# Two-layer diffusion backbone: context row gathers held beside the first layer's pair selection and table, and 72 in place of 56 u chunks ahead of the dense stage

## The chip, the cores and the metric

The kernel runs on one core of one Trainium2 chip. Its engines are TensorE (PE), VectorE (DVE), ScalarE (ACT) and GpSimd (POOL); SyncE (SP) issues most transfers. The metric is device time in microseconds for one execution of the whole program.

## The reference, cut to what matters

512 latent tokens and 256 context tokens of width 1024 go through two layers. Each layer is a mixer (attention, a gating MLP, Fourier mixing, gates), then an expert retrieval. The second layer's attention reads keys and values of the context too, so it needs what the context's retrieval in the first layer gives.

```python
q = rms_unit((t @ w_q).reshape(T, 8, 2, 128))
s = einsum('thpc,hpkc->thpk', q, sub_keys)
s1, i1 = top_k(s[:, :, 0], 16); s2, i2 = top_k(s[:, :, 1], 16)
# 256 pairs of each head -> the best 16 pairs: idx = i1 * 128 + i2, g = softmax(scores)
act = gelu(einsum('td,thkd->thk', t, u_tab[idx]))
out = einsum('thk,thkd->td', g * act, v_tab[idx])     # 16384 rows of 1024 in each table
```

## The kernel before

**Two ways to do the retrieval.** For the first layer's 512 latent tokens the kernel does it densely: all 128 chunks of 128 table rows are multiplied with the tokens (`dense_u`, then gelu), the result is multiplied with a table of pair weights that `gtable` writes to DRAM, and the product goes through the 128 chunks of v (`dense_v`). For the 256 context tokens it gathers rows instead: two blocks of 128 tokens with 128 pairs each, first all rows of u, then all rows of v. These are four jobs (block 0 u, block 0 v, block 1 u, block 1 v) of 128 steps.

**How gathers are paced.** `step()` (L836) issues one indirect transfer of 128 rows (512 KB) on POOL's queue into one of four row buffers and, three steps later (LAG), uses a row on DVE: a product summed into a column of dots for u (L867), a multiply-add into acc for v (L876). Each use is tied behind the DVE instruction that was the latest when it was traced. `pace(cols)` (L827) is called behind every group of three matmuls and adds cols / 2.4 ns to `owed`; each 1700 ns of it is one step. `spend()` (L833) takes 1800 ns away for each 512 KB tile loaded (0.4 of that for a spilled chunk read back), down to -7200. `finish()` (L881) issues all steps that are left at once.

**Order of the first layer's expert part.** `interleave` (L145) advances generators in rounds. Here they are: the second layer's conditioning columns (`ada`, 24 loads, 0.4 a round), the rest of the context's routing (`cr`), `routing()` (1 a round: 8 rounds of norm, 8 of `route1`, one for each head, and 32 of `route2`, 8 for each of four blocks), `table()` (1 a round; block b starts when `route2` has done it, so its 32 rounds begin in the last round of the first block and end 7 rounds after `route2`), and `fill()` (FILL[0] a round, once the norm is done). `fill()` makes u chunks ahead of the dense stage: SPILL[0][0] + NGS - LEAD of them, 40 + 16 - 2 = 54; two more follow before the dense loop, 56 in all. Forty of the 56 are spilled: written to DRAM (`gsd`) and read back in `dense_v`. SPILL[0] = (40, 3) spills every third chunk. What `fill()` has not made when the rounds end, it makes alone. The dense loop then makes 128 v chunks and the other 72 u chunks, one behind each v chunk that is not a spilled one.

**The second layer.** Its mix (Fourier, then the gating MLP: 36 rounds) is interleaved with `context()` (L1085), with the gates of two branches (16 weight tiles, 0.6 a round) and with 16 conditioning loads (1.2 a round). `context()` waits until the last context row is used or mix has ended; then it calls `finish()`, adds the rows' sum to the context, norms it and writes ctx.H and ctx.L. Behind the interleave comes `qkv` (L503), with K first: `projN` (L350) loads four weight tiles and multiplies each with the four latent blocks, whose accumulators fill all four ps banks, and with the two context blocks (px banks). The split weight tiles have three buffers.

Of the kernel before, what the change touches and what calls it, by code (L numbers as in the profile page):

```python
# [47 lines left out]
STEPS = ((1700, 1700, 1700), (1700, 1700, 1700))  # L48
LAG = 3
NGSS = (16, 30)  # L50
SPILL = ((40, 3), (40, 3))
FILL = (1.0, 1.3)
LEAD = 2
ADA = 6
WBUFS = ((3, 2), (3, 4))
# [22 lines left out]
class Ker:  # L78
    def __init__(self, tc, a, es):
        self.tc, self.nc, self.a, self.es = tc, tc.nc, a, es  # L80
        self.uid, self.turn, self.banks = 0, False, PBANKS
        self.wp = self.wb = self.wr = None
        self.jobs, self.flight, self.owed, self.every = [], [], 0, STEPS[0][0]


    def pool(self, es, name, bufs=1, space=None, side=None):
# [738 lines left out]
        self.jobs.append({"l": l, "r": r, "tab": tab, "next": 0})  # L825

    def pace(self, cols):  # L827
        self.owed += cols / 2.4
        while self.owed >= self.every:
            self.owed -= self.every  # L830
            self.step()
# [103 lines left out]
    @staticmethod  # L935
    def spilled(l, c):
        n, m = SPILL[l]
        return c % m == m - 1 and c // m < n

    def dense_u(self, l, c, sp, up, hH, hL, tag, bufs):  # L940
# [9 lines left out]
        if spill:  # L950
            nc.sync.dma_start(self.gsd[c // SPILL[l][1]], gS)
        return gS

    def dense_v(self, l, c, vp, sp, gS, gd, accs, acc7, between):
# [12 lines left out]
        if self.spilled(l, c):  # L967
            gS = vp.tile([P, TD], F32, tag="gSr", name=self.nm("gSr"), bufs=2)
            nc.sync.dma_start(gS, self.gsd[c // SPILL[l][1]])
            self.spend(0.4)  # L970
# [28 lines left out]
    def layer(self, l, xin, cin, xfin, rin):  # L999
        nc, a, tc, two = self.nc, self.a, self.tc, self.two  # L1000
        last = l == DEPTH - 1
# [5 lines left out]
        gd = dt("gd", [TD // GT, P, NK * GT])  # L1007
        self.gsd = dt("gsd", [SPILL[l][0], P, TD])
        cm = cfin = None
# [173 lines left out]
        def ahead(n):  # L1183
            while len(gSs) < n:
                c = order[len(gSs)]
                gSs[c] = self.dense_u(l, c, self.pp, up, dH, dL, "ps", self.banks["ps"])
                yield
        with ExitStack() as e:
            rp = self.pool(e, f"rp{l}")
            for b in range(4):  # L1190
                for n in ("i1", "i2", "g"):
                    if n not in rx[b]:
                        rx[b][n] = rp.tile([P, P], F32, name=f"{n}x{l}_{b}")
            gt, normed = [], []

            def routing():
                with ExitStack() as e2:
                    tmp = self.pool(e2, f"rn{l}")
                    yield from self.norm(tmp, l, xm, SEQ, 1, 0, lambda k: (dH[:, k, :], dL[:, k, :]), r1)
                    normed.append(True)  # L1200
                with ExitStack() as e2:
                    tmp = self.pool(e2, f"rt{l}")
                    yield from self.route1(l, tmp, rp, SimpleNamespace(H=dH, L=dL, T=SEQ), (tmp, *PQB))
                with ExitStack() as e2:
                    tmp = self.pool(e2, f"nat{l}")
                    for b in range(NDB, 4):
                        self.natural(tmp, rx[b]["hnd"], dH, dL, b)
                gt.append(self.pool(e, f"gt{l}"))
                yield from self.route2(gt[0], list(range(NDB, 4)) + list(range(NDB)), rx, l)

            def table():
                for b in range(NDB):
                    while "done" not in rx[b]:
                        yield
                    yield from self.gtable(gt[0], b, rx[b], gd)

            def fill():
                while not normed:
                    yield
                yield from ahead(SPILL[l][0] + NGS - LEAD)  # L1220
            self.interleave((self.ada(*((l, range(10, 12)) if last else (l + 1, range(ADA))), None, "fl"), 4 * AN[l]),
                            (None if last else cr, CR2), (routing(), 1), (table(), 1), (fill(), FILL[l]))
        epp.close()

        self.every = STEPS[l][2]
        with ExitStack() as e:
            vp = self.pool(e, f"dv{l}")
            acc7 = vp.tile([P, TD], F32, name=f"da{l}_7")
            with ExitStack() as e2:
# [3 lines left out]
                self.added = {}  # L1233
                room = [SPILL[l][0] + NGS]

# [170 lines left out]
```

## Time and profile before

| | us |
|---|---|
| median of three runs | 4993.69 |
| lowest run | 4987.19 |
| the profiled execution | 4982.3 |
| its span, from first to last instruction | 4980.5 |

Shares of the span: PE 91%, DVE 68%, POOL 41%, ACT 38%. The chain that ended last is PE for 57%, DVE 15%, DMA 8%. The first layer's expert part runs from about 1100 to 2895 us, and the second layer's mix from 2947 to 3148. Matmul ends are modelled and successive matmuls overlap, so the spacing of matmuls says more than their mean length. In the rows, du and d, da are the matmuls of the u and v chunks, px of the table (and the context's accumulators in the second layer), idxc the indices of the context's rows.

### The profile page before, as it was taken

What the parts mean: (1) busy time and instruction counts of PE and PEld (TensorE: products, weight loads), DVE (VectorE), ACT (ScalarE), POOL (GpSimd) and SP (SyncE); (2) the same over time, 40 slices, a digit from 0 to 9 for tenths busy, and PEclk for the clock granted to TensorE, in tenths of its full rate; (3) what the DMA queues carried; (4) which work ended last, traced back from release to release, by engine and by line L of the source; (5) the groups of instructions that cost most, each with busy time, mean ns of one, the idle gap of its engine ahead of it and who ended that gap; (6) DMA issues with size and microseconds to landing.
All of it is one profiled execution on the core that took longest, in us unless ns stands there. A gap on an engine that the chain in (4) does not pass through costs nothing.

```text
span 4980.5 us, 65298 instructions
## 1 busy us (share of the span) xinstructions
PE 4521.8 (91%) x23501; PEld 3851.7 (77%) x23501; DVE 3366.8 (68%) x6818; ACT 1910.4 (38%) x3201; POOL 2029.4 (41%) x1246
## 2 busy tenths in 40 slices
PE   7899988789789899999899989989897899999998
PEld 4787777667667788877778767767787788999998
DVE  3115485868888667766777874457459976777787
ACT  2222444322578522222222233334334783333332
POOL 1011012335655565655556420111225665555531
PEclk9999999989999999999999999999999899999999
DMA  4442245556567889988889886333536668888986
GB/s 167 144 135 68 92 134 167 170 174 217 200 223 247 297 285 318 318 290 273 272 294 303 306 267 204 101 96 110 170 92 192 214 241 297 293 289 301 302 287 228
DMA packets 447508, 1092.84 MB, mean 219 GB/s; under 512 B 37200, under 2 KB 193744, under 8 KB 440016
## 3 DMA queue, kind: packets, MB, share of 16 engines
q1 hardware_dynamic: 336592, 685.97, 42.2%
q0 software_dynamic: 110592, 402.70, 23.6%
q8 instruction: 185, 3.03, 0.2%
q14 instruction: 139, 1.14, 0.1%
HBM read 970.04 MB, written 118.49 MB: 219 GB/s over the span
## 4 chain that ended last, share of the span: by engine, by line
PE 57%; DVE 15%; issue 8%; DMA 8%; POOL 5%; ACT 4%; SPq 0%; POOLq 0%; DVEq 0%; ACTq 0%
PE du L113 6%; PE du L115 5%; PE du L114 5%; PE da L114 5%; PE da L113 5%; PE da L115 5%; PE ps L113 3%; PE ps L114 3%; PE ps L115 3%; DMA row<-in_u_dram,idxc 2%; POOL row L848 2%; PE px L929 2%; DVE row L867 2%; PE px L113 2%; PE px L115 2%
## 5 line engine op out<-in xcount | busy, mean ns | idle before, releaser
L109 POOL TENSOR_TENSOR wL<-wraw,wH 128x1024 fp32r<-128x1024 f32 x291 | 714.9, 2458 | 1138.9 <-ACT wH L102 1053.4
L102 ACT ACTIVATE wH<-wraw 128x1024 fp32r<-128x1024 f32 x460 | 486.7, 1059 | 1155.2 <-PE du L114 319.5
L113 PE MATMUL du<-dH,wH 128*128 128x512 f32 (+1 forms) x2048 | 781.5, 382 | 64.5 <-DVE da L990 45.5
L115 PE MATMUL du<-dH,wL 128*128 128x512 f32 (+1 forms) x2048 | 774.1, 378 | 43.8 <-DVE wL L109 22.6
L114 PE MATMUL du<-dL,wH 128*128 128x512 f32 (+1 forms) x2048 | 769.5, 376 | 6.5 <-DVE dL L335 6.5
L113 PE MATMUL da<-AH,vH 128*128 128x512 f32 (+1 forms) x1792 | 647.3, 363 | 7.8 <-ACT AH L102 7.8
L114 PE MATMUL da<-AL,vH 128*128 128x512 f32 (+1 forms) x1792 | 651.1, 363 | 0.7 <-DVE AL L109 0.6
L115 PE MATMUL da<-AH,vL 128*128 128x512 f32 (+1 forms) x1792 | 650.5, 363 | 0.0
L867 DVE SCALAR_TENSOR_TENSOR row<-row,hn 128x1024 f32<-128x1024 f32 x384 | 508.6, 1345 | 103.6 <-DMA row<-in_u_dram,idxc 89.8
L102 ACT ACTIVATE vH<-vr 128x1024 fp32r<-128x1024 f32 x256 | 271.7, 1062 | 779.6 <-PE da L114 550.1
L876 DVE SCALAR_TENSOR_TENSOR acc<-row,dots,acc 128x1024 f32<-128x1024 f32 x381 | 501.2, 1315 | 7.6 <-DMA row<-in_v_dram,idxc 3.7
L113 PEld LDWEIGHTS du<-dH,wH 128*128 128x128 f32 x2048 | 399.9, 195 | 123.1 <-DVE da L990 56.2
L848 POOL DMA_INDIRECT row<-in_v_dram,idxc x256 | 327.8, 1280 | 406.1 <-DVE acc L876 354.7
L115 PEld LDWEIGHTS du<-dH,wL 128*128 128x128 f32 x2048 | 400.2, 195 | 94.2 <-DVE wL L109 27.1
L848 POOL DMA_INDIRECT row<-in_u_dram,idxc x256 | 334.2, 1305 | 324.1 <-DVE row L867 228.4
L114 PEld LDWEIGHTS du<-dL,wH 128*128 128x128 f32 x2048 | 400.0, 195 | 47.5 <-DVE dL L335 9.0
L109 DVE TENSOR_TENSOR wL<-wraw,wH 128x1024 fp32r<-128x1024 f32 x169 | 220.8, 1307 | 269.0 <-ACT wH L102 256.4
L990 DVE TENSOR_TENSOR da<-d,da 128x512 f32<-128x512 f32 (+1 forms) x254 | 158.1, 622 | 333.3 <-PE d L115 332.8
L113 PEld LDWEIGHTS da<-AH,vH 128*128 128x128 f32 x1792 | 337.8, 189 | 43.9 <-ACT AH L102 8.5
L114 PEld LDWEIGHTS da<-AL,vH 128*128 128x128 f32 x1792 | 338.0, 189 | 37.7 <-DVE AL L109 2.4
L115 PEld LDWEIGHTS da<-AH,vL 128*128 128x128 f32 x1792 | 338.0, 189 | 35.3
L109 DVE TENSOR_TENSOR vL<-vr,vH 128x1024 fp32r<-128x1024 f32 x256 | 326.2, 1274 | 50.9 <-ACT vH L102 49.2
(385 smaller groups left out, 9441.9 us busy)
## 6 DMA issues: line engine op xcount, KB each, us to landing
wraw<-in_uT_dram SPq DMA_DIRECT2D x256, 512.0 KB, 4.6
vr<-in_v_dram SPq DMA_DIRECT2D x256, 512.0 KB, 6.1
wraw<-in_wt_dram SPq DMA_DIRECT2D x204, 512.0 KB, 3.7
gd<-stg SPq DMA_DIRECT2D x56, 1024.0 KB, 5.4
araw<-in_wada_dram SPq DMA_DIRECT2D x96, 512.0 KB, 4.4
gt<-gd SPq DMA_DIRECT2D x16, 2048.0 KB, 18.0
gt<-gd SPq DMA_DIRECT2D x16, 1536.0 KB, 12.4
gatex<-g SPq DMA_DIRECT2D x48, 256.0 KB, 2.1
```

What stands on the lines that cost most here:

```text
L102: nc.scalar.activation(H, src, AF.Copy)
L109: e.tensor_tensor(L, src, H.bitcast(F32), op=ALU.subtract)
L113: nc.tensor.matmul(out, aH, bH, start=start, stop=False)
L114: nc.tensor.matmul(out, aH, bL, start=False, stop=False)
L115: nc.tensor.matmul(out, aL, bH, start=False, stop=stop)
L848: nc.gpsimd.indirect_dma_start(out=row, out_offset=None, in_=self.a[f"{job['tab']}{job['l']}"], in_offset=bass.IndirectOffsetOnAxis(ap=r[" ...
L867: nc.vector.scalar_tensor_tensor(row, row, 1.0, job["hn"], op0=ALU.mult, op1=ALU.mult, accum_out=dots[:, j:j + 1])
L876: nc.vector.scalar_tensor_tensor(job["acc"], row, dots[:, j:j + 1], job["acc"], op0=ALU.mult, op1=ALU.add)
L929: nc.tensor.matmul(gp[:, j * P:(j + 1) * P], ob[:, j, :], oa[:, j, :], start=True, stop=True)
L990: add = nc.vector.tensor_tensor(acc7, s[:, :TD], acc7, op=ALU.add)
```

## The change

- While `held` is set, `pace` returns at once: nothing is added to `owed` and no step is issued; `spend` still takes away. It is set in the first layer when `route1` is done, and cleared when the last table block is traced. The second layer doesn't hold.
- SPILL[0] goes from (40, 3) to (56, 2): every second chunk is spilled, 56 in all, so `fill()` makes 56 + 16 - 2 = 70 chunks, with two more before the loop; 56 u chunks are left for the loop.
- FILL[0] goes from 1.0 to 1.3 chunks a round.

```diff
--- before.py
+++ after.py
@@ -48,8 +48,8 @@
 STEPS = ((1700, 1700, 1700), (1700, 1700, 1700))
 LAG = 3
 NGSS = (16, 30)
-SPILL = ((40, 3), (40, 3))
-FILL = (1.0, 1.3)
+SPILL = ((56, 2), (40, 3))
+FILL = (1.3, 1.3)
 LEAD = 2
 ADA = 6
 WBUFS = ((3, 2), (3, 4))
@@ -81,6 +81,7 @@
         self.uid, self.turn, self.banks = 0, False, PBANKS
         self.wp = self.wb = self.wr = None
         self.jobs, self.flight, self.owed, self.every = [], [], 0, STEPS[0][0]
+        self.held = False
 
 
     def pool(self, es, name, bufs=1, space=None, side=None):
@@ -825,6 +826,8 @@
         self.jobs.append({"l": l, "r": r, "tab": tab, "next": 0})
 
     def pace(self, cols):
+        if self.held:
+            return
         self.owed += cols / 2.4
         while self.owed >= self.every:
             self.owed -= self.every
@@ -1205,6 +1208,7 @@
                     tmp = self.pool(e2, f"nat{l}")
                     for b in range(NDB, 4):
                         self.natural(tmp, rx[b]["hnd"], dH, dL, b)
+                self.held = not last
                 gt.append(self.pool(e, f"gt{l}"))
                 yield from self.route2(gt[0], list(range(NDB, 4)) + list(range(NDB)), rx, l)
 
@@ -1213,6 +1217,7 @@
                     while "done" not in rx[b]:
                         yield
                     yield from self.gtable(gt[0], b, rx[b], gd)
+                self.held = False
 
             def fill():
                 while not normed:
```

## Rows read from the trace of the kernel before

**Rows 1.** The page, busy us of each engine, share of the span and instructions:

```profile
PE 4521.8 (91%) x23501; PEld 3851.7 (77%) x23501; DVE 3366.8 (68%) x6818; ACT 1910.4 (38%) x3201; POOL 2029.4 (41%) x1246
```

**Rows 2.** Windows: stretch, length, busy us (instructions) by engine, granted clock, DMA, GB/s:

```profile
1100.00:1237.00 137.00, 125.10 (x620) 102.21 (x619) 110.56 (x481) 40.07 (x69) 79.60 (x50) 0.95 0.66 212
1237.00:1673.00 436.00, 373.48 (x2053) 294.27 (x2052) 378.47 (x886) 312.69 (x610) 257.25 (x153) 0.95 0.67 229
1673.00:2895.00 1222.00, 1168.16 (x5041) 953.51 (x5040) 883.23 (x1064) 336.12 (x426) 692.56 (x463) 0.98 0.88 297
...
2947.00:3148.00 201.00, 189.30 (x1011) 151.31 (x1010) 93.72 (x165) 68.08 (x108) 12.91 (x12) 0.97 0.64 207
```

**Rows 3.** Windows of the context's row gathers alone, on POOL, columns alike:

```profile
980.00:1237.00 257.00, 59.71 (x46) 0.90 0.60 193
1237.00:1673.00 436.00, 76.01 (x59) 0.95 0.67 229
1673.00:2895.00 1222.00, 501.85 (x386) 0.98 0.88 297
2895.00:3040.00 145.00, 24.39 (x22) 0.91 0.77 257
```

**Rows 4.** Timeline of POOL, the last context gathers: start us, length us, instruction [idle]:

```profile
3030.40 1.87 POOL L848 DMA_INDIRECT row<-in_v_dram,idxc  x1 [0.59 <-DVE acc L876]
3032.57 1.01 POOL L848 DMA_INDIRECT row<-in_v_dram,idxc  x1 [0.30 <-issue]
3033.89 1.58 POOL L848 DMA_INDIRECT row<-in_v_dram,idxc  x1 [0.30 <-issue]
3035.77 0.94 POOL L848 DMA_INDIRECT row<-in_v_dram,idxc  x1 [0.30 <-issue]
```

**Rows 5.** Windows of the dense stage: v rows, u rows of block two, v rows:

```profile
1775.00:2150.00 375.00, 375.00 (x1656) 310.50 (x1655) 279.65 (x295) 109.35 (x140) 226.11 (x156) 1.00 0.91 314
2175.00:2575.00 400.00, 360.41 (x1512) 290.03 (x1510) 280.38 (x394) 101.22 (x127) 228.20 (x148) 0.97 0.83 275
2600.00:2750.00 150.00, 150.00 (x664) 124.20 (x663) 112.03 (x118) 43.18 (x55) 92.61 (x64) 1.00 0.92 317
```

**Rows 6.** Groups by line, 1237 to 1673 us: count, busy us, mean ns, idle before:

```profile
L113 PE MATMUL du<-dH,wH 128*128 128x512 f32 x294 | 124.2, 422 | 0.3 <-ACT wH L102 0.3
...
L867 DVE SCALAR_TENSOR_TENSOR row<-row,hn 128x1024 f32<-128x1024 f32 x59 | 73.8, 1275 | 2.8 <-DMA row<-in_u_dram,idxc 2.8
```

**Rows 7.** Timeline of PE, fourteen table matmuls in a row:

```profile
1501.84 1.83 PE L929 MATMUL px<-oa,ob 128*128 128x128 f32 x14
```

**Rows 8.** Tile dots, its gelu: ns min/median/max, first and last start us:

```profile
L869 ACT ACTIVATE dots<-dots x2: 292/292/292, 1783.3 to 2587.0; 128x128 f32<-128x128 f32 x2
```

**Rows 9.** Tile row, 2895 to 3060 us, columns alike, and landing times:

```profile
L876 DVE SCALAR_TENSOR_TENSOR acc<-row,dots,acc x25: 1275/1280/1336, 2897.1 to 3042.0; 128x1024 f32<-128x1024 f32 x25
...
DMA to landing us min/median/max: 4.4/6.3/8.8
```

**Rows 10.** Timeline of POOL, two of the first gathers:

```profile
984.82 0.95 POOL L848 DMA_INDIRECT row<-in_u_dram,idxc  x1 [0.30 <-PE ps L115]
986.08 0.95 POOL L848 DMA_INDIRECT row<-in_u_dram,idxc  x1 [0.31 <-issue]
```

**Rows 11.** Tiles acc and hL of the context, 3036 to 3130 us, columns alike:

```profile
L878 SPq DMA_DIRECT2D accdc<-acc x1: 327/327/327, 3043.3 to 3043.3; - x1
...
L335 DVE SCALAR_TENSOR_TENSOR hL<-nt,mod,hH x8: 479/484/488, 3094.5 to 3110.5; 128x256 fp32r<-128x256 f32 x8
```

**Rows 12.** Timeline of DVE, the last operation of mix:

```profile
3147.48 0.69 DVE L644 TENSOR_TENSOR ct<-ct,cu 128x512 f32<-128x512 f32 x1
```

**Rows 13.** Timeline of ACT, splits of K's weight tiles and what ended the wait:

```profile
3153.69 1.06 ACT L102 ACTIVATE wH<-wraw 128x1024 fp32r<-128x1024 f32 x1 [7.75 <-PE px L115]
3161.85 1.06 ACT L102 ACTIVATE wH<-wraw 128x1024 fp32r<-128x1024 f32 x1 [7.10 <-PE px L115]
3170.01 1.06 ACT L102 ACTIVATE wH<-wraw 128x1024 fp32r<-128x1024 f32 x1 [7.10 <-PE px L115]
```

## The prediction

> **What bounds the kernel now.** I read the page's busy shares first: TensorE (PE) is busy for 91% of the span [rows 1], so time is mostly won by closing its gaps, and work that only moves from one place to another on PE wins nothing unless it falls into a gap. Next I cut the first layer's expert part and the start of the second layer into stages [rows 2]. Route 1 (1100 to 1237 us) has 12 us of PE gaps. Pair selection and table (1237 to 1673) is the loosest stage: PE 373 of 436 us, VectorE (DVE) 378. The rest of the dense stage (1673 to 2895) is PE at 96%. Mix in the second layer (2947 to 3148) is PE at 94%, with DVE under half used. Then I counted the context's gathered rows by stage [rows 3]: 46 before the pair selection, 59 beside it and the table, 386 until the dense stage ends, 22 in the second layer, the last of them issued at 3035.77 us [rows 4], far ahead of the end of mix. The context chain waits for the last row, and today nobody waits for the context.
>
> **The account of the rows.** This is where the change has its largest effect, and it can be done by hand. A weight or table tile of 24 matmuls of 512 columns earns 24 x 512 / 2.4 = 5120 ns and its load costs 1800, so it earns 3320 ns, or 1.95 steps of 1700 ns. A spilled chunk read back costs 720 more. The four context jobs need 512 steps to issue and 3 more to use the last rows: 515.
> Kernel before: after the table there are 7 + 2 + 72 u chunks and 128 v chunks, so (209 x 3320 - 40 x 720) / 1700 = 391 steps; the trace shows 386 issues [rows 3]. The account holds within 2%.
> After: fill runs at 1.3 per round instead of 1, which adds 2.4 u chunks to the 8 rounds of route 1: 46 + 4 = 50 steps ahead of the hold. In the hold there are none, while loads go on being charged, so the credit ends at its floor of -7200 ns (-4 steps). The 39 rounds of the hold make about 51 u chunks instead of 39; 61 instead of 47 are done by its end. Then come 9 + 2 + 56 u chunks and 128 v chunks, with 56 read back: (195 x 3320 - 56 x 720) / 1700 = 357, less 4 for the floor and 2 for two conditioning loads that still come: 351. So 401 of 515 steps are done when the second layer starts; 114 are left, against 22 shown today.
> What mix can take: 12 weight tiles (39.8 us of credit), the Fourier products, which charge no load (25.6), 16 gate tiles (53.1), less 16 conditioning loads (28.8): 89.7 us, or 53 steps. That leaves 61. When mix ends, context() calls finish(), which issues all 61 in one go, and only then come the residual, the norm and ctx.H.
>
> **The change part by part.**
> Fewer u chunks behind the table: 209 - 195 = 14 chunks. With PE packed, 1656 matmuls take 375 us, or 0.2264 us each [rows 5], so a chunk is 5.43 us and 14 are 76 us less there.
> The same chunks beside routing: 2.4 of them (13 us) in route 1, which has 12 us of gaps; between 0 and 13, I take 7. In the hold there are 12 more. Today PE needs there 294 / 8 = 36.75 chunks [rows 6], 200 us, and 1024 table matmuls. Fourteen of these end 1.83 us after the first starts, with the last one's 0.27 us in it [rows 7], so they are 0.12 us apart, 123 us in all. With 13 us of conditioning and transposes it is 336 of 436 us. After it is 401. DVE loses 59 uses with 73.8 us [rows 6] and goes from 378 to about 305, plus 7 for six more splits; it stops being the tightest engine. The stage then lies between 401 us (PE packed) and 472 (PE used to 85%); I take 437, the middle, which is no change.
> More u rows in the dense stage: with the u rows of a block PE does 1512 matmuls in 400 us, where packed it would do 1767; with v rows it is packed [rows 5]. The last use of the second block's u rows is just ahead of the second gelu of the dots at 2587 us [rows 8], so this stretch holds its 128 rows. It loses 255 x 0.2264 = 58 us, or 0.45 us for each u row. The 55 u rows that move here from the table (206 instead of 151) cost 25 us. The bounds are 0 and 35, should the denser mix of v chunks make it worse. The v rows that leave for the second layer give nothing back, since they cost nothing.
> Extra spills: 16 more stores and 16 more reads of 256 KB against 16 fewer 512 KB tiles in that stage. The queue gets lighter; costed at nothing. What hides it is that DMA stands at 0.88 there [rows 2]; without that cover it would be some 0.7 us for each read at the 0.9 and more that the v stretches show [rows 5], so 11 us.
> The 53 rows paced through mix: 1.28 us of DVE each [rows 9] beside a DVE used 94 of 201 us [rows 2]; nothing, at most 10 us.
> The burst of 61 steps. Each gather waits for one of four row buffers, so the spacing is a quarter of release, issue, landing and use. The nearest row is the end of the last job today, with all four buffers turning: three intervals from 3030.40 to 3035.77, 1.79 us each [rows 4], at landings of 4.4 to 8.8 us [rows 9]. The floor is the spacing of issues that wait for nothing, 1.26 us [rows 10]; the ceiling is the paced spacing of the dense stage, 1222 / 386 = 3.17 us [rows 3]. So 61 steps cost 110 us, between 77 and 193.
> One rule speaks for less. The row shows a median landing of 6.3 us for a 512 KB gather [rows 9]. The Trainium skill, page DMA: Bandwidth & Descriptors, section Anatomy of one DMA, fits a transfer from that queue as 2.0 us plus bytes over 436 GB/s, an estimate of 3.2 us for these rows. By that the burst would turn at about 1.28 us a step and cost 78 us, and the total would be 31 us less than mine; the trace has no landing under 4.4 us in that stretch, so I keep the row.
> The chain behind the burst, read off today's: the sum is written at 3043.3 and the first hL of the context is there at 3094.5 us [rows 11]: 51 us. The burst starts behind the last DVE operation of mix, 3147.5 [rows 12], since each use is tied behind the latest DVE instruction. PE is last fed by the K projection: each tile does 24 latent matmuls, then 12 of the context. Three tiles fit the split buffers; today each new split waits for the context's matmuls (px) of an earlier tile [rows 13]. So PE can do at most three latent parts, 16 us from about 3145.2, and stands from 3161.7 on. Its gap is 3147.5 + 110 + 51 - 3161.7 = 147 us; with one part only, 158.
>
> **The sum.** 4980.5 - 76 + 7 + 0 + 25 + 147 = 5083.5 us of span: 44 us won up to the end of the dense stage, 147 lost in mix's wake. The profiled execution was 4982.3 us, 1.8 over its span, and the median of the runs is 11.4 above that, so a median would be 5097.
>
> **The rivals.**
> Filled gap (ends on the other side, no slower): PE's order could put other matmuls ahead of the context's part: eight tiles of the first branch's gates, the latent parts of Q and V, and the fourth of K, 93 us. The gap is then 54 us and the time 4993.7 + 54 - 44 = 5004; below 44 us of gap it decides for no loss. Against it: K's four accumulators hold all four ps banks until its last context matmul, and the splits wait on px [rows 13].
> The table stage falls with DVE: if it is the 78 us of uses that set it, it goes to 358 us. With the gap this is 5097 - 78 = 5019. Against it: PE alone needs 401 there.
> Slow burst: the rows come at the paced 3.17 us, because landing under other loads sets them. 84 us more, 5181. For it: the landings of up to 8.8 us; against it: in the burst nothing but four weight tiles shares the queues.
> Hold without backlog: the account of credit is wrong and the rows are done before mix ends. Then only the 44 us of gain stay: 4950. Against it: the account gives today's 386 within 5.
>
> **How the numbers follow.** About 2% (100 us here) is what a measurement of this kernel can tell from no change, and my forecast of +103 stands right on that line. The forecast with its own range (5030 to 5150: gain 0 to 80, burst 77 to 140): 0.66, of which 0.40 above the line. Filled gap: 0.14, all within 2%. Table falls: 0.05, within. Slow burst: 0.11, slower. No backlog: 0.04, split evenly. This gives faster 0.02, same 0.47, slower 0.51; I move 0.01 to faster for gains not listed. The range runs from 4990 to 5185 and leaves out the no-backlog case and the far end of the slow burst.
>
> **What would show it.** In the profile after: no context gathers between pair selection and table end, some 350 from there to the end of the dense stage, 50 paced in mix, and then 55 to 60 in one block spaced 1.7 to 1.9 us, with PE idle for 130 to 160 us before the context's part of K, waiting at the end for the context's hL. The stage of selection and table within 400 to 470 us; the second block's u stretch again near 90% PE. Wrong if the last context row is issued before mix ends, or if PE works on gates or Q while the burst runs.

## The result, and the profile after

The changed kernel takes 5097.88 us (median of four runs, 5083.82 to 5101.18) against 4988.27 before: a ratio of 1.0219, with a 95% interval of 1.0203 to 1.0235. One of the four runs of the kernel before took 11380.49 us and is left out of these figures. The change makes the kernel slower by 2.2%, and 5097 was forecast. The profiled execution has a span of 5081.9 us, 101.4 more than before. Lines of `kernel.py` below 84 have moved down by one, those behind `pace` by three.

The stages come first, as the windows of all engines show them: selection and table, the rest of the dense stage, mix, and a stretch that had no counterpart before. The columns are those of [rows 2].

```profile
1246.00:1729.00 483.00, 434.71 (x2362) 345.18 (x2361) 324.50 (x780) 330.78 (x635) 182.58 (x102) 0.97 0.48 167
1729.00:2835.00 1106.00, 1078.95 (x4706) 881.47 (x4705) 833.25 (x1087) 315.70 (x398) 615.21 (x412) 0.99 0.91 308
2887.00:3091.00 204.00, 188.48 (x991) 151.81 (x990) 110.55 (x140) 60.81 (x91) 57.62 (x45) 0.97 0.78 260
3097.00:3261.00 164.00, 10.08 (x26) 4.77 (x24) 89.62 (x101) 3.65 (x10) 74.49 (x61) 0.51 0.68 221
```

Against [rows 2], selection and table take 483 us instead of 436, and the rest of the dense stage takes 1106 instead of 1222. Then, behind mix, PE does next to nothing for 164 us. The windows of the context's gathers alone answer to [rows 3]:

```profile
980.00:1246.00 266.00, 59.06 (x47) 0.90 0.60 194
1246.00:1729.00 483.00, 1.18 (x2) 0.97 0.48 167
1729.00:2835.00 1106.00, 462.04 (x350) 0.99 0.91 308
2835.00:3090.00 255.00, 68.30 (x54) 0.93 0.77 257
3090.00:3206.00 116.00, 73.63 (x60) 0.55 0.81 268
```

The account had said 50, none, 351, 53 and 61 steps; the last three steps of all use a row and issue none, so 61 steps are 58 gathers. The two issues inside the hold are steps that earlier credit paid for, and 60 gathers are issued behind mix. The view of the tile row in this last stretch answers to [rows 9]:

```profile
L879 DVE SCALAR_TENSOR_TENSOR acc<-row,dots,acc x61: 1280/1285/1322, 3090.8 to 3205.9; 128x1024 f32<-128x1024 f32 x61
...
DMA to landing us min/median/max: 4.9/5.7/6.4
```

And the chain of work that ended last, its longest pieces in the same stretch, in order of time:

```profile
3111.80 5.25 DMA row<-in_v_dram,idxc
3120.93 1.57 POOL row L851
3126.65 6.05 DMA row<-in_v_dram,idxc
...
3213.20 2.60 DMA accdc<-acc
3216.28 6.64 DMA rx<-cm
3237.18 3.48 DMA cfin<-rx
3241.11 2.18 DMA nx<-cfin
```

The chain runs through landings and issues of rows, then the sum's way through DRAM, the residual and the norm. PE's timeline shows the other side: K's latent part ends with the matmul at 3096.91 us, and the context's first one starts at 3261.43.

```profile
3096.91 0.39 PE L116 MATMUL ps<-wH,hL 128*128 128x512 f32 x1
...
3261.43 0.79 PE L114 MATMUL px<-wH,hH 128*128 128x512 f32 x1 [1.53 <-ACT hH L335]
```

Marks read from the tile views of each profile give the whole difference. Selection starts 11.4 us later (1233.9 to 1245.3). Selection and table take 43.8 more (439.9 to 483.7, up to the last store of the table). The dense stage takes 116.2 less up to its last v matmuls. Mix takes 3.7 more. From the last operation of mix to the context's part of K (its first matmul with L) it is 172.7 us instead of 3.7. Behind that 10.3 come back. Of these, 4.9 lie in the rest of K (35.7 us instead of 40.6), where two tiles' latent parts are already done instead of one. The other 5.4 lie behind K, where the twelve profiles of this document spread from 1779 to 1797 us without any order, so nothing is read from them. 11.4 + 43.8 - 116.2 + 3.7 + 169.0 - 10.3 = 101.4.

### The profile page after: what moved, and what is told of

Read it like the earlier page. It is cut to its first block, busy times and chain, and to the rows that moved or that the text cites. A ratio compares the mean times of both kernels' runs of the same rounds, so it can differ in the third digit from the quotient of the medians.

```text
span 5081.9 us, 65451 instructions
## 1 busy us (share of the span) xinstructions
PE 4507.2 (89%) x23501; PEld 3835.2 (75%) x23501; DVE 3392.0 (67%) x6826; ACT 1910.9 (38%) x3201; POOL 1993.5 (39%) x1238
## 4 chain that ended last, share of the span: by engine, by line
PE 41%; DVE 7%; DMA 7%; issue 6%; POOL 2%; ACT 2%; SPq 0%; POOLq 0%; ACTq 0%; DVEq 0%
PE da L115 6%; PE da L114 6%; PE da L116 6%; PE du L114 4%; PE du L116 4%; PE du L115 4%; DMA row<-in_v_dram,idxc 2%; POOL row L851 1%; DVE row L870 1%; DMA row<-in_u_dram,idxc 1%; PE ps L114 1%; PE ps L115 1%; PE ps L116 1%; PE px L932 1%; PE d L114 1%
## 5 line engine op out<-in xcount | busy, mean ns | idle before, releaser
L110 POOL TENSOR_TENSOR wL<-wraw,wH 128x1024 fp32r<-128x1024 f32 x283 | 699.1, 2471 | 1277.8 <-ACT wH L103 1058.5
```

Of the source, the lines that this page charges most:

```text
L110: e.tensor_tensor(L, src, H.bitcast(F32), op=ALU.subtract)
```

## The experiments

The theory: the loss is the burst of rows behind mix with the chain after it, and it depends only on how many steps the credit has paid for by then; all else in the change is a gain of some 60 us. The rivals: the new order of chunks with its spills costs time; PE waits for something other than rows; or rows could be taken in elsewhere at no cost. The table has the marks of every run from its profile, in us (the start of selection, the end of the table, of the dense stage and of mix, and the context's first matmul with L in K), then the steps that the account, taken up again after the result, leaves when mix ends (62 for the changed kernel, where the prediction had 61), and the measured ratio. Apart from the changed kernel all runs lie within 2% of the kernel before; where the interval of the ratio leaves out 1, the text calls the run faster or slower.

| run | selection | table | dense | mix | K, context | steps left | ratio to before |
|---|---|---|---|---|---|---|---|
| before | 1234 | 1674 | 2897 | 3147 | 3151 | 0 | |
| after | 1245 | 1729 | 2836 | 3090 | 3263 | 62 | 1.0219 |
| chunks only | 1244 | 1738 | 2844 | 3094 | 3093 | 0 | 0.9874 [0.985, 0.9898] |
| hold only | 1231 | 1638 | 2887 | 3135 | 3246 | 32 | 1.0168 [1.014, 1.0196] |
| burst cut | 1245 | 1729 | 2843 | 3093 | 3147 | 3 | 0.9982 [0.9969, 0.9995] |
| 1350 ns a step | 1248 | 1734 | 2967 | 3212 | 3215 | 0 | 1.0132 [1.0104, 1.016] |
| six buffers | 1232 | 1716 | 2813 | 3056 | 3209 | 64 | 1.0113 [1.0095, 1.0131] |
| order only | 1236 | 1675 | 2876 | 3123 | 3127 | 0 | 0.9953 [0.9936, 0.997] |
| fill at 1.0 | 1229 | 1636 | 2835 | 3078 | 3203 | 39 | 1.0088 [1.0072, 1.0105] |
| chunks, six buffers | 1232 | 1727 | 2821 | 3068 | 3072 | 0 | 0.9815 [0.9799, 0.9831] |
| six buffers, 1350 ns | 1233 | 1717 | 2904 | 3151 | 3155 | 0 | 0.9992 [0.9982, 1.0002] |
| before, six buffers | 1227 | 1666 | 2864 | 3107 | 3110 | 0 | 0.9892 [0.9874, 0.9909] |

**The change without the hold.**

```diff
-                self.held = not last
+                self.held = False
```

> The changed kernel without the hold: every second chunk spilled, 72 chunks ahead, 1.3 a round, but the context rows go on beside selection and table. Mine (the loss is the burst of rows behind mix): by the account 487 of 515 steps are done when the second layer starts, so the last row is used well before mix ends, no burst and no PE gap; the dense stage keeps most of its 116 us, selection and table grow from 436 us by 48 or more, since the rows' uses stay there. 4930 to 4975 us, a ratio of 0.987 to 0.998. Rival (the denser order of v chunks with more spills is what costs): it stays at 5050 to 5100 us.

Measured: 4916.82 us, faster than before by 1.3%. It was 13 us below the expected stretch. The dense stage keeps its whole gain (1107 us from the end of the table, as in the changed kernel, against 1224 before), and from the end of mix on this run takes 14 us less than the kernel before, which no run explains. The context's matmuls in K follow mix at once, and the new order with its spills costs nothing. What the changed kernel loses, it loses through the hold.

**The hold alone**, with SPILL and FILL as before.

```diff
-SPILL = ((56, 2), (40, 3))
-FILL = (1.3, 1.3)
+SPILL = ((40, 3), (40, 3))
+FILL = (1.0, 1.3)
```

> The kernel before with the hold alone: 40 spilled, 56 chunks ahead, 1.0 a round. Mine: 430 steps done when the second layer starts, 483 when mix ends, so a burst of 32 rows at 1.88 us and the chain behind it of 48 us: a PE gap of about 100 us. Selection and table fall by 30 to 50 us, since DVE loses 78 us of uses and PE needs 336 of 436; the 59 rows that move into the dense stage cost it up to 25. Sum 5030 to 5075 us, a ratio of 1.01 to 1.017. Rival (the table stage is bound by DVE's uses, and the context is off the path): 4910 to 4940, faster than before.

Measured: 5070.3 us. Selection and table do fall, from 440 to 407 us, as the uses leave DVE. But the stretch from the table's end to the end of the dense stage grows by 26 us with the moved u rows, and the gap behind mix is 112 us. The windows of the context's gathers behind mix show 30 issues where the account leaves 32 steps:

```profile
3134.80:3192.30 57.50, 35.05 (x30) 0.59 0.81 275
```

**The burst left out.** `cut` takes the place of `finish` in `context()`:

```diff
-                self.finish(rc[1])
+                self.cut(rc[1])
+    def cut(self, r):
+        nc = self.nc
+        if "summed" in r:
+            return
+        self.jobs = []
+        while self.flight:
+            job = self.flight[0][0]
+            self.step()
+        nc.sync.dma_start(r["accd"], job["acc"])
+        r["summed"] = True
```

> The changed kernel, but the rows of the last job that are not issued when mix ends are left out: the three in flight are used, the sum is written, the rest is not gathered (part of the context's retrieval is left out). Mine: the burst of about 58 rows at 1.88 us, 110 us, goes, the chain of 48 us behind it stays: 4980 to 5000 us. Rival (PE waits for something else than the rows, such as the norm or weight tiles): 5080 to 5100, unchanged.

Measured: 4978.9 us, 119 less than the changed kernel's median and 1 us below the stretch expected. The gap falls to 54 us, which is the chain from the last row to the context's H and L. So PE did wait for rows. With the other runs this gives their price: (172.7 - 53.7) / (62 - 3) = 2.0 us a row, and the hold alone (111.7 - 53.7) / 29 and fill at 1.0 (125.7 - 53.7) / 36 give 2.0 as well.

**More rows in the dense stage.**

```diff
-STEPS = ((1700, 1700, 1700), (1700, 1700, 1700))
+STEPS = ((1700, 1700, 1350), (1700, 1700, 1700))
```

> The changed kernel with a step each 1350 ns of credit in the dense stage instead of 1700: by the account 488 steps are done when the second layer starts, as in the kernel before, and the last row is used in the middle of mix. Mine: the PE gap of 164 us goes; the dense stage takes 88 more rows in, 117 us more of DVE work beside 833 of 1106, and grows by 0 to 40: 4930 to 4975 us, a ratio of 0.987 to 0.997. Rival (the dense stage has no room for them: DVE or DMA sets it): it gives back 80 us or more there, 5015 or later.

Measured: 5044.96 us, the rival's result. The gap is gone, and the dense stage gives 126 us back (1234 instead of 1108 from the end of the table), 1.4 us for each of its 87 more rows. Windows of the dense loop, the changed kernel first and then this run:

```profile
1797.00:2837.00 1040.00, 1019.07 (x4443) 834.34 (x4441) 802.05 (x1043) 297.00 (x373) 580.01 (x392) 0.99 0.91 307
```

```profile
1802.00:2967.00 1165.00, 1053.19 (x4442) 843.40 (x4442) 986.73 (x1131) 303.86 (x373) 686.36 (x479) 0.98 0.91 313
...
PEld du L114 <- DVE da L993: 81.2, 43, 3.9
PE du L114 <- DVE da L993: 63.5, 40, 3.5
DVE row L870 <- DMA row<-in_u_dram,idxc: 52.4, 52, 3.3
DVE acc L879 <- DMA row<-in_v_dram,idxc: 39.5, 43, 3.7
```

The number of matmuls is the same. The waits (who waited for whom: us, times, longest) show u matmuls waiting for DVE's additions of d7, and DVE for rows still on their way, v rows too. At 1700 ns the v rows cost nothing (the 384 us of the first block's v rows hold all the matmuls that fit but 2 us); at 1350 they no longer fit beside the matmuls (39 us lost in the 338 of the same rows).

**Six row buffers** instead of four in the first layer (the places that use `LAG` take the layer's value).

```diff
-LAG = 3
-NGSS = (16, 30)
-SPILL = ((56, 2), (40, 3))
+LAG = (5, 3)
+NGSS = (12, 30)
+SPILL = ((60, 2), (40, 3))
```

> The changed kernel with six row buffers instead of four in the first layer (a row is used five steps after its issue); for their room 60 chunks are spilled and 12 kept, 72 ahead as before. Mine (in the burst each row waits for one of four buffers to turn): the cycle of 7.5 us is shared by six, 1.25 us, so the spacing falls from 1.88 to the 1.3 to 1.4 us that POOL's issue and DVE's use allow; the gap shrinks by 30 to 36 us: 5050 to 5070 us. Rival (the DMA engines set the burst, 0.83 busy in it): spacing stays near 1.88, 5085 to 5105.

Measured: 5035.57 us, below the stretch. The burst's share is smaller than expected: the gap falls by 20 us, to 153, although two more rows are in it. Another 34 come earlier: selection starts 13 us sooner, the dense stage and mix take 10 to 11 us less each. Rows are awaited there too, but this run, which also keeps four chunks fewer, does not show that this is the reason everywhere. Windows and tile view of the burst:

```profile
3057.00:3152.00 95.00, 6.49 (x29) 5.05 (x27) 81.26 (x66) 0.00 (x0) 71.34 (x62) 0.56 0.92 336
```

```profile
L851 POOL DMA_INDIRECT row<-in_v_dram,idxc x62: 941/1019/1882, 3058.7 to 3151.5; - x62
its engine sat idle before it (us, times) until:
  DVE acc L879: 25.1, 3
  issue: 17.7, 58
```

The issues are 92.8 / 61 = 1.52 us apart. POOL is busy issuing for 71 of the 95 us and sits another 17.7 us in front of 58 issues with nothing awaited. By this view it is mostly POOL's issuing that sets the pace with six buffers, with the DMA engines at 0.92 close behind; no run separates the two.

**The order of the chunks**: every second of the first 80 chunks spilled instead of every third of 120, on the kernel before.

```diff
-SPILL = ((40, 3), (40, 3))
+SPILL = ((40, 2), (40, 3))
```

> The kernel before with every second of the first 80 chunks spilled instead of every third of 120: still 40 spilled and 56 ahead, 1.0 a round, no hold. Tests why the stretch of u rows lost 58 us in the kernel before and only about 12 after the change. If the order of u and v chunks in the dense loop does it (one u for two v instead of two for three): the stretch of the second block's u rows loses 10 to 25 us, 4940 to 4965 us. Rival (the smaller number of u chunks in the loop, or the moved rows, does it): it loses 50 to 60 as before, 4980 to 4995.

Measured: 4959.74 us, a gain of 0.5%. This run tests the order within itself. The loop does one u for two v chunks for the first 80 v chunks, 122 chunks of 5.43 us, so until about 2410 us, and one u for each v after that, while u rows of the second block are used on both sides. PE windows before and after that point:

```profile
2200.00:2400.00 200.00, 192.49 (x838) 156.48 (x839) 154.92 (x225) 55.06 (x69) 114.03 (x76) 1.00 0.90 305
2400.00:2575.00 175.00, 159.09 (x665) 127.95 (x664) 125.78 (x165) 44.97 (x57) 99.51 (x69) 0.96 0.81 271
```

Packed would be 883 and 773 matmuls: the first part loses 5%, the second 14%, as the kernel before did with two u for three v [rows 5]. So with one u for two v the same rows cost least. Together the two parts lose 35 us, above the 10 to 25 that were expected, because the new order ends in the middle of the stretch. In the changed kernel the whole stretch of these rows loses 24 us, not the 12 that the expectation names.

**Fill at 1.0** in the changed kernel.

```diff
-FILL = (1.3, 1.3)
+FILL = (1.0, 1.3)
```

> The changed kernel with fill at 1.0 a round: selection and table make 39 u chunks instead of 51, and 23 are made alone behind the table instead of 9. Mine (selection and table grow by PE's work of the twelve chunks, not by anything of the rows): this stage falls from 484 to 400 to 415 us, the tail grows by 76, and about 39 rows instead of 62 are left when mix ends, 44 us less gap: 5040 to 5065 us. Rival (the stage is set by ACT or DVE and stays at 470 to 485): 5110 or later.

Measured: 5026.0 us, 14 below the stretch. Selection and table fall from 484 to 406 us as expected, so the twelve chunks are what made them grow, at 77 / 12 = 6.4 us each. The gap falls by 47.

**The change without the hold, and six buffers.** The edits of the first experiment and of the six buffers together.

> Without the hold, 72 chunks ahead (60 spilled, 12 kept), and six row buffers. Mine (what is left of the loss beside u rows is DVE waiting for a row that has not landed): the dense stage loses a further 10 to 20 us, 4895 to 4912 us. Rival (the rows land in time already): 4912 to 4925, as with four buffers.

Measured: 4889.19 us, faster than the kernel before by 1.9% and than the changed one by 4%; it is the fastest of all. Beside the second block's u rows PE is now next to packed, 1494 matmuls of 1502 in 2180 to 2520 us, and from the first of these rows to the last 5 us are lost:

```profile
2180.00:2520.00 340.00, 339.28 (x1494) 279.87 (x1493) 266.03 (x394) 100.91 (x125) 208.95 (x134) 1.00 0.93 319
```

**Six buffers with 1350 ns a step.** The edits of both.

> The changed kernel with six row buffers and a step each 1350 ns of credit in the dense stage: the run with 1350 and four buffers lost its PE gap and gave 130 us back in the dense stage. By the account some 485 steps are done when the second layer starts, so no gap. If the dense stage lost that time by waiting for rows that had not landed: it falls from 1165 to 1040 to 1080 us, and the time to 4890 to 4935. If the DMA engines or DVE have no room for 87 more rows: it stays at 1120 to 1170 us, and the time at 4975 to 5040.

Measured: 4983.5 us, the second answer at its lower edge: the dense loop falls from 1165 to 1119 us, against 1029 with six buffers at 1700.

```profile
1790.00:2900.00 1110.00, 1025.07 (x4400) 825.71 (x4399) 996.69 (x1119) 300.09 (x369) 713.72 (x471) 0.99 0.94 326
```

So the two buffers win back 35 of the 125 us that the 87 rows cost there with four. Waits for landings are not the rest: DVE waits 5.9 us for u rows in this loop and none for v rows, where with four buffers it was 52.4 and 39.5. DVE is busy for 90% and the DMA engines for 94%. The trace shows something else as well. In this loop 50 DVE instructions take over 0.3 us more than the median of their kind, 125 us in all, and each of them overlaps one of POOL's 56 subtractions that make the low half of a u tile (wL). At 1350 ns with four buffers there are 49 of them with 97 us, in the changed kernel 13 with 16, with six buffers at 1700 seven with 13. One of them on DVE's timeline, and the subtraction on POOL's:

```profile
1996.71 4.20 DVE L879 SCALAR_TENSOR_TENSOR acc<-row,dots,acc 128x1024 f32<-128x1024 f32 x1
...
1997.40 2.42 POOL L110 TENSOR_TENSOR wL<-wraw,wH 128x1024 fp32r<-128x1024 f32 x1
```

The same use of a row takes 1.28 us otherwise. No run moves this subtraction, so which of DVE's work, this overlap and the DMA engines sets the remaining 90 us is left open.

**Six buffers on the kernel before**, with 42 chunks spilled and 12 kept, 54 ahead.

> The kernel before with six row buffers (42 spilled and 12 kept, so 54 ahead instead of 56; neither hold nor 1.3 a round). If the 58 us that the second block's u rows cost in the dense stage come from uses that wait for a landing and hold up the additions behind them: they fall to 0 to 15 us and the time to 4925 to 4950. If they come from the order of the chunks alone: 4970 to 4990.

Measured: 4931.86 us, a gain of 1.1%. In 2150 to 2500 us PE does 1441 matmuls where 1546 would fit: 24 us lost. From the first of the second block's u rows to the last (2178 to 2558 us) it is 28, instead of 59 in the kernel before (2169 to 2585).

```profile
2150.00:2500.00 350.00, 331.87 (x1441) 271.32 (x1441) 265.58 (x369) 96.19 (x120) 214.16 (x138) 0.99 0.89 302
```

The waits beside these rows, in the kernel before and then in this run:

```profile
DVE row L867 <- DMA row<-in_u_dram,idxc: 50.2, 26, 5.1
PE du L113 <- DVE da L990: 34.4, 15, 4.6
...
DVE row L867 <- DMA row<-in_u_dram,idxc: 0.4, 2, 0.2
```

Both answers hold in part. Rows that have not landed go with about half of the loss, and with six buffers DVE hardly waits for them. The order of the chunks goes with as much: with the changed kernel's order and four buffers 24 us are lost, and with both changes (the change without the hold, six buffers) 5. So the two are not separate shares of the 59; late rows cost PE most where the order of the chunks leaves little room.

## Why the prediction was right, and which steps of it were off

**The account of the rows.** Right. 351 steps in the dense stage were forecast and 350 issues found; 53 in mix and 54 found; 61 steps behind mix, that is 58 gathers, and 60 gathers found. In three other runs the gathers behind mix were two fewer than the steps that the account leaves (30 for 32, 62 for 64, 37 for 39). This decided the case, since the price of a row differs by place: beside the table it costs DVE 1.3 us, in the dense loop at 1700 ns nothing to 0.45, behind mix 2.0 of the path.

**The burst and the chain behind it.** Right in kind, 17 us too small. PE idles 164 us where 147 were forecast. From the end of mix to the end of the last use it is 123 us, 1.98 a step, where 1.79 was taken from three intervals of [rows 4]. The chain from there to the context's matmuls is 48 us where today's 51 were taken. K's latent part ran ahead for two tiles, not three: 11 us instead of 16. The Trainium skill's fit (DMA: Bandwidth & Descriptors, Anatomy of one DMA) would have given an estimate of 3.2 us for a landing. The burst, with hardly anything else on the queues, shows 4.9 to 6.4. The measurement decides, and the row was the better price. The run with six buffers shows why the landing counts: four buffers share its cycle.

**The table stage.** Wrong: no change was forecast, within 401 to 472 us, and it took 484 (+44). The failed step is "I take 437, the middle". A chunk of u between table matmuls costs 6.4 us, not the 5.43 of a packed one, and the 78 us of uses that left DVE did not pay for twelve of them: with the chunks, the hold wins 9 us in this stage (493 to 484), without them 33 (440 to 407). What sets this stage then is not shown: PE is busy for 90% of it, DVE, ACT and POOL for less than 70%.

**The u rows in the dense stage.** Wrong in sign. 0.45 us for each u row was carried over as if it were a price of the row, and 25 us were added. With the new order the second block's u rows cost 24 us instead of 59 (2412 to 2804 us; in the 350 us from 2425 PE does 1459 matmuls where 1546 would fit), and the dense stage won 116 us instead of 51. PE is busy for 96% there, not again near 90% as the prediction expected. The price belonged to the order of chunks in which it was read, as the run with the order alone shows within one trace, and to four row buffers, as the run with six in the kernel before shows.

```profile
2425.00:2775.00 350.00, 336.34 (x1459) 275.18 (x1458) 267.89 (x394) 99.38 (x124) 190.63 (x128) 0.99 0.90 302
```

**The sum** hit because these cancel: 44 us too little in the table and 4 in route 1, 65 too much in the dense stage, and the gap 12 too small net of the work done ahead, with 4 in mix. The forecast of the place and kind of the loss was right; the exact total was luck. So was the step from a profiled execution to a median: 11.4 us were taken from three runs; the changed kernel's median is 14.1 above its profiled execution, and the kernel before's later medians (4981.65 to 4988.4) lie 1 below to 6 above its own.

**The rivals.** The filled gap did not happen: PE's timeline holds no gates and no Q in the burst. The slow burst (3.17 us) did not happen; rows came at 1.98. The table stage did not fall with DVE. The backlog was there.

## What to carry to other kernels

When background work is paced by credit that foreground work earns, a hold or less foreground work doesn't make it cheaper; it moves it to the next point that needs it done. Count the steps to that point by hand before moving anything: here the count found 61 steps on the path, and one line undone turned a loss of 2.2% into a gain of 1.3%. And a price read in one stretch (0.45 us a row) is a price of that order of work and of that number of buffers; if the change alters either, don't carry it over. Here the whole range of 0 to 35 us that was added for it lay on the wrong side.

## What the runs showed of the hardware that had not been expected

Two more row buffers in flight were worth nearly as much as the change without its hold (1.1% and 1.3%): the kernel before gains 1.1% by them, with four kept chunks given up for their room, and the changed one without its hold goes from 0.9874 to 0.9815. With four buffers DVE waited 26 times for the second block's u rows, 50.2 us in all, and u matmuls waited 34.4 us for DVE's additions of d7, which share a bank with them. That is how a late landing reached PE; the view of waits names DVE as the one that PE waits for, and only DVE's own line names the row.

DVE instructions that overlap POOL's subtraction of a split tile can take three times as long (4.2 us for a use of 1.28), 125 us in the dense loop with six buffers at 1350 ns. The profile counts this time as busy DVE.

In the burst, gathers of 512 KB with four in flight moved 268 GB/s at a DMA share of 0.81, with six 336 at 0.92. And PE's granted clock in the 164 us gap, where it is busy for 10 us, is 0.51, the lower of its two levels (1.2 of 2.4 GHz); from 3262 to 3350, where it is busy for 82 of 88 us, it is 0.97.
